# Attention scores of a two-layer trunk: q and k in rounded hi/lo parts, or in plain fp32 on either half of the partitions

## The chip, the cores and the metric

The kernel runs on one core of a Trainium2 chip. The metric is the device time of one execution in microseconds (us); lower is better. A change under about 2% can't be told from no change with certainty.

## What is computed

A decoder trunk of two layers on one sequence of 1024 positions with model width 1024, all in fp32. Layer 0 mixes tokens by a gated MLP in chunks, layer 1 by attention; each is followed by a squared-ReLU MLP of width 4096. The change is in the attention, of which this is the core (16 heads of width 64; three branches g, each with its own q, k and v; window and dilation (128, 1), (512, 4), (2048, 16)):

```python
def dilated_branch(q, k, v, window, dilation, slopes):
    span = window // dilation
    ...
    qb = to_blocks(q)
    kb = with_prev(to_blocks(k))        # the block before and the block itself
    vb = with_prev(to_blocks(v))
    s = jnp.einsum('bnqrhe,bnkrhe->bnrhqk', qb, kb,
                   preferred_element_type=jnp.float32) * (E ** -0.5)
    ...
    s = s + bias
    s = jnp.where(valid[None, :, None, None], s, NEG)
    m = jnp.max(s, axis=-1, keepdims=True)
    p = jnp.exp(s - m)
    l = jnp.sum(p, axis=-1, keepdims=True)
    o = jnp.einsum('bnrhqk,bnkrhe->bnqrhe', p / l, vb.astype(jnp.float32))
    lse = (m + jnp.log(l))[..., 0].transpose(0, 1, 4, 2, 3)
```

The span is 128 positions in each branch. The three outputs are then weighted by a softmax over their `lse` and added.

## The kernel before, in words

**Number formats.** Large products run in the rounded format fp32r. To keep precision, an operand is split: `split(hi, lo, src)` (L100) lets ScalarE (ACT) write the rounded part `hi` (L102) and VectorE (DVE) the remainder `lo = src - hi` (L103). A product is then three matmuls, hi·hi, hi·lo and lo·hi.

**The stages.** `mixer_a`, `mlp(1)`, `attention`, the output rows, and `mlp(3)` follow one another. The two MLPs take most of the time (L782, L938).

**The attention stage** handles 8 head pairs `hp`, and for each the branches g = 2, 1, 0: 24 groups. Two streams of work are woven together.

- `project()` is a generator. For each group it computes q, k and v of the head pair for the two halves of the positions, into PSUM banks of kind `mm` (two). For each of 8 k-steps it issues three 512-column matmuls (L1134) and yields. After the last k-step the bank, which holds the pair's two heads on partitions 0 to 63 and 64 to 127, is evicted: v by a copy on ACT (L1141), q and k by the lines that change. Positions are reordered by `perm` and `by_pos`, so that each branch finds its blocks side by side.
- `attend(n, …)` puts the attention work of a group into slots, eight to a group, four for each head `e`. `scores(m)` treats query tiles 2m and 2m+1 of 128 queries each. A tile sees its own 128 keys, and also the 128 before where `has[t]` is true (256 keys): all tiles but the first in branch 0, the odd tiles in branch 1, none in branch 2. The scores lie in PSUM banks of kind `sc` (two). DVE adds the bias and takes the row minimum of the negated scores (L1214), ACT takes the exponential and the sum (L1216). `transposes(m)` turns the probabilities by TensorE (L1239, L1242) and splits them; `weighted(m)` multiplies them with v (L1262), and ACT and DVE evict the sums (L1279, L1280).

The main loop goes through the slots. A slot has two parts, scores with weighted values, and transpositions; behind each part come three steps of `project()`, nine 512-column matmuls. When the projections are used up, in the last group, the first steps of the output projection (`begin`) take their place. The framework orders instructions by a planner of its own, except those that are pinned by `keep_in_program_order`.

**q and k before.** For each head `e` there are tiles `q{e}`, `k{e}` of 128 partitions in fp32r, two buffers each, and four fixed tiles `qlo[e][b]`. With the head's own 64 partitions called `mine` and the others `other`, `k{e}` holds hi on `mine` and lo on `other`; `q{e}` holds hi on `mine`, and GpSimd (POOL) copies it to `other` when both halves are there (L1150); `qlo` holds lo on `mine` and zeros on `other`, cleared once at the start (L1064). A score tile is two matmuls over all 128 partitions into one group: `q{e}` with `k{e}` (L1207) gives hi·hi + hi·lo, and `qlo` with `k{e}` (L1208) gives lo·hi. Both tiles of a `scores(m)` lie in one bank, side by side.

Of the kernel before, what the change touches and what calls it, by code (L numbers as in the profile page):

```python
# [10 lines left out]
F32 = mybir.dt.float32  # L11
F32R = mybir.dt.float32r
AF = mybir.ActivationFunctionType
ALU = mybir.AluOpType
# [3 lines left out]
P = 128  # L18
S = 1024
# [16 lines left out]
def trunk(ctx: ExitStack, tc: tile.TileContext, x, c, ada_w, ada_b, ln_g, ln_b, a_w_in, a_b_in,  # L36
# [4 lines left out]
    V, A, G, T = nc.vector, nc.scalar, nc.gpsimd, nc.tensor  # L41

    def pool(stack, name, bufs, **kw):
        return stack.enter_context(tc.tile_pool(name=name, bufs=bufs, reuse_waits="tile", **kw))
# [52 lines left out]
    def bank(kind, name):  # L97
        return ps[kind].tile([P, HALF], F32, name=name, tag=kind)

    def split(hi, lo, src, hi_engine=A, lo_engine=V):  # L100

        first = A.copy(hi, src) if hi_engine is A else hi_engine.tensor_copy(hi, src)  # L102
        return first, lo_engine.tensor_tensor(lo, src, hi, op=ALU.subtract)  # L103
# [943 lines left out]
    def attention(before):  # L1047
# [6 lines left out]
        with ExitStack() as ph:  # L1054
            open_psum(ph, "B", sc=2, pv=2, mm=2, tr=2)
            vec = pool(ph, "vecB", 1)
            gate = row_tile(gate_dram[2], "gate_2", "gate")
            ql = pool(ph, "attn_qlo", 1)
            qk = pool(ph, "attn_qk", 2)
            qp = pool(ph, "attn", 2)  # L1060
            qlo = [[ql.tile([P, S], F32R, name=f"qlo{e}_{b}") for b in range(2)] for e in range(2)]
            for e in range(2):
                for b in range(2):
                    (V if b else G).memset(qlo[e][b][64 - 64 * e : P - 64 * e, :].bitcast(F32), 0.0)  # L1064


            near = qp.tile([P, 2 * P], F32, name="near", bufs=1)
            G.iota(near[:], pattern=[[-1, 2 * P]], base=P, channel_multiplier=1, allow_small_or_imprecise_dtypes=True)
# [8 lines left out]
            def perm(t, g, half=None):  # L1077

                d = DILATION[g]
                if g == 0:  # L1080
                    return t if half is None else t[:, half * HALF : (half + 1) * HALF]
                if g == 1:
                    v = t.rearrange("p (r i) -> p r i", r=d)
                    n = v.shape[2] // 2
                else:
                    v = t.rearrange("p (a b i) -> p a b i", b=2, i=S // d)
                    n = v.shape[3] // 2
                return v[..., half * n : (half + 1) * n]

            def by_pos(t, g):  # L1090

                if g == 0:
                    return t
                if g == 1:
                    return t.rearrange("p (i r) -> p r i", r=4)
                return t.rearrange("p (i b a) -> p a b i", b=2, a=8)

            order = [(hp, g) for hp in range(N_PAIRS) for g in (2, 1, 0)]
            got = [dict() for _ in order]

            def project():

                todo = [(n, X) for n in range(len(order)) for X in range(3)]
                parts = [(n, X, half) for half in (1, 0) for n, X in todo[:4]]
                parts += [(n, X, half) for n, X in todo[4:] for half in (1, 0)]
                build = before.build(0)

                def load(n, X):
                    hp, g = order[n]
                    c0 = g * 3 * D + X * D + hp * P  # L1110
                    return unit(b_w_qkv[0, :, c0 : c0 + P], f"w{'qkv'[X]}_{hp}_{g}")

                units = {key: load(*key) for key in todo[:4]}
                for n, X, half in parts:
                    if (n, X, half) == (0, 0, 0):
                        run(build)
                    hp, g = order[n]
                    nm = "qkv"[X]
                    i = 3 * n + X
                    if half == 1 and 3 <= i < len(todo) - 1:  # L1120
                        units[todo[i + 1]] = load(*todo[i + 1])
                    if half == 1:
                        if nm == "v":
                            got[n]["vT"] = vec.tile([P, S], F32, name=f"vT_{hp}_{g}", tag="lnb")
                        else:
                            if nm == "q":
                                got[n]["qlo"] = [qlo[e][n % 2] for e in range(2)]
                            for m in ((f"{nm}0", f"{nm}1")):
                                got[n][m] = qk.tile([P, S], F32R, name=f"{m}_{hp}_{g}", tag=m)
                    wu = units[n, X]  # L1130
                    p = bank("mm", f"ps{nm}_{hp}_{g}_{half}")
                    for k in range(KD):
                        for c_, (a, b) in enumerate(((0, 0), (0, 1), (1, 0))):
                            T.matmul(p[:], wu[a][:, k * P : (k + 1) * P], hT[half][b][:, k, :],  # L1134
                                     start=k + c_ == 0, stop=k == KD - 1 and c_ == 2)
                        if half == 1 and (n, X) in ((0, 2), (1, 0)) and k % 2:
                            next(build, None)
                        if k == KD - 1:
                            src = by_pos(p[:], g)
                            if nm == "v":  # L1140
                                A.copy(perm(got[n]["vT"][:], g, half), src)  # L1141
                            else:
                                for e in range(2):
                                    mine, other = slice(64 * e, 64 * e + 64), slice(64 - 64 * e, P - 64 * e)
                                    t = got[n][f"{nm}{e}"]
                                    hi = perm(t[mine, :], g, half)
                                    lo = perm(got[n]["qlo"][e][mine, :] if nm == "q" else t[other, :], g, half)
                                    split(hi, lo, by_pos(p[mine, :], g))
                                    if nm == "q" and half == 0:
                                        G.tensor_scalar(t[other, :], t[mine, :], 1.0, 1.0, ALU.mult, ALU.mult)  # L1150
                        yield


# [14 lines left out]
            def attend(n, oT_of):  # L1168
                hp, g = order[n]
                base = 8 * n  # L1170
                my = got[n]
                has = [(g == 0 and t > 0) or (g == 1 and t % 2 == 1) for t in range(NT)]
                width = P if g == 2 else 2 * P
# [12 lines left out]
                for e in range(2):  # L1186
                    h = 2 * hp + e
                    rows = slice(e * HEAD, (e + 1) * HEAD)
                    probs, pvs, st = {}, [], dict(begun=[False, False])

                    def scores(m, e=e, h=h, rows=rows, probs=probs, st=st):
                        if m == 0:
                            if e == 0:
                                my["stat"] = qp.tile([P, 2, 2, NT], F32, name=f"stat_{hp}_{g}", tag="stat", bufs=3)
                            st["bias"] = qp.tile([P, width], F32, name=f"bias_{h}_{g}", tag="bias")
                            G.tensor_scalar(st["bias"][:], (far if g == 2 else near)[:],
                                            -8.0 * DILATION[g] * 2.0 ** (-8.0 * (h + 1) / N_HEADS), 1.0, ALU.mult, ALU.mult)
                        scb, used = bank("sc", f"sc_{h}_{g}_{m}"), 0
                        stat = my["stat"]
                        spans = []  # L1200
                        for t in (2 * m, 2 * m + 1):
                            w = 2 * P if has[t] else P
                            sl = slice(used, used + w)
                            used += w
                            k0 = (t - 1) * P if has[t] else t * P
                            tq, keys = slice(t * P, (t + 1) * P), my[f"k{e}"]
                            T.matmul(scb[:, sl], my[f"q{e}"][:, tq], keys[:, k0 : k0 + w], start=True, stop=False)  # L1207
                            T.matmul(scb[:, sl], my["qlo"][e][:, tq], keys[:, k0 : k0 + w], start=False, stop=True)  # L1208
                            spans.append((t, w, sl))
                        for t, w, sl in spans:  # L1210
                            pr = qp.tile([P, 2 * P], F32, name=f"p_{h}_{g}_{t}", tag="p", bufs=4)
                            col = (t % 2) * 4 + t // 2 if g == 1 else t
                            nm, l = stat[:, 0, e, col : col + 1], stat[:, 1, e, col : col + 1]
                            V.tensor_tensor_reduce(out=pr[:, 0:w], in0=scb[:, sl], in1=st["bias"][:, width - w :], scale=-0.125, scalar=3e38,  # L1214
                                                   op0=ALU.add, op1=ALU.min, accum_out=nm)
                            A.activation(pr[:, 0:w], pr[:, 0:w], AF.Exp, bias=nm, scale=-1.0, accum_out=l)  # L1216
                            probs[t] = pr
# [216 lines left out]
    out = attention(done)  # L1434
# [31 lines left out]
```

## Time and profile before

| | |
|---|---|
| time, two runs | 2842.47 and 2847.93 us, median 2845.2 |
| profiled execution, first to last instruction | span 2841.6 us (its own time is not given apart) |
| TensorE (PE) busy | 2752.7 us, 97% |
| VectorE (DVE), ScalarE (ACT) busy | 1944.5 us, 1413.9 us |
| first and last score matmul | 1045.3 and 2115.3 us |
| score matmuls, L1207 and L1208 | 384 and 384 |

The page gives the busy time of each engine, its share of 40 slices of the span, the chain of work that ended last and the costliest groups of instructions. PE is the matmul stream and PEld the weight loads beside it; matmul durations overlap, so a matmul's price is read from the distance between two starts. In a group, "out<-in" names tiles by the program's names, then come rows*columns of the weights, the shape, the count, busy us and mean ns of one, and the idle time before with what ended it. In a line in order of time, the first number is the start, the second the duration, both in us.

### The profile page before, as it was taken

Reading aid. Unit: us, or ns where it says so; the run is one execution under the profiler, and the core shown is the slowest. Engines: PE = TensorE matmul, PEld = TensorE weight load, DVE = VectorE, ACT = ScalarE, POOL = GpSimd, SP = SyncE. Lnnn points to the kernel's source line nnn. Section 1 sums busy time; section 2 is a strip of 40 time slices with the busy share of each in tenths; the row PEclk is TensorE's granted clock in tenths of the full one; section 3 lists DMA queues with packets and bytes.
Section 4 is the critical chain, followed back from the end, with each engine's and each line's share of the span. In section 5 each row is a group of like instructions: output and inputs, shape, how many; then the busy total and the mean of one; then the engine's idle time right before and its main releaser. Section 6 shows DMA issues by size and latency. Waiting matters only on the chain.

```text
span 2841.6 us, 36856 instructions
## 1 busy us (share of the span) xinstructions
PE 2752.7 (97%) x13290; PEld 2277.9 (80%) x13290; DVE 1944.5 (68%) x3485; ACT 1413.9 (50%) x2613; POOL 220.1 (8%) x163
## 2 busy tenths in 40 slices
PE   6999999999999999999999999999999999999997
PEld 5777878887888878888888888888877788878886
DVE  6786798777877674656555555555659976577776
ACT  3334375555434455555555555555564755544431
POOL 1021000000000043101000000010201000000000
PEclk9999999999999999999999999999999999999999
DMA  7533346668846343212121212121315564485561
GB/s 253 171 109 106 119 152 223 216 219 277 286 153 201 126 148 105 61 39 68 38 61 39 69 31 69 38 69 31 91 39 178 170 208 158 151 303 189 171 214 60
DMA packets 300186, 384.15 MB, mean 135 GB/s; under 512 B 47532, under 2 KB 172884, under 8 KB 300004
## 3 DMA queue, kind: packets, MB, share of 16 engines
q1 hardware_dynamic: 300004, 381.80, 42.0%
q8 instruction: 104, 1.70, 0.2%
q14 instruction: 78, 0.64, 0.1%
HBM read 297.77 MB, written 83.97 MB: 134 GB/s over the span
## 4 chain that ended last, share of the span: by engine, by line
PE 73%; DVE 11%; DMA 7%; ACT 5%; issue 2%; POOL 2%; SPq 0%; DVEq 0%; ACTq 0%; POOLq 0%
PE psd L938 21%; PE psua L782 10%; PE psv L1134 8%; PE psq L1134 7%; PE psk L1134 5%; PE psuc L782 5%; DMA adaw<-in_ada_w_dram 3%; PE psd_wout L356 3%; PE psub L782 2%; PE pv L1262 2%; PE psd_wo L356 2%; ACT p L1216 1%; DVE adaacc L128 1%; PE psu L356 1%; PE sc L1208 1%
## 5 line engine op out<-in xcount | busy, mean ns | idle before, releaser
L782 PE MATMUL psua<-right,left 128*128 128x512 f32 x1536 | 364.0, 391 | 3.4 <-ACT right L102 1.8
L938 PE MATMUL psd<-rhi,lhi 128*128 128x512 f32 x896 | 351.0, 392 | 2.1 <-ACT part L813 2.1
L938 PE MATMUL psd<-rlo,lhi 128*128 128x512 f32 x896 | 350.9, 392 | 1.2 <-DVE rlo L103 1.1
L938 PE MATMUL psd<-rhi,llo 128*128 128x512 f32 x896 | 350.5, 391 | 0.0
L782 PEld LDWEIGHTS psua<-right,left 128*128 128x128 f32 x1536 | 287.3, 188 | 65.5 <-DVE right L103 3.1
L1216 ACT ACTIVATE p<-p,stat 128x128 f32<-128x128 f32 (+1 forms) x384 | 170.4, 445 | 237.6 <-DVE stat L1214 235.7
L1134 PE MATMUL psv<-hT,wv_hi 128*128 128x512 f32 x768 | 246.0, 401 | 3.2 <-DVE qlo L103 3.2
L1134 PE MATMUL psq<-hT,wq_hi 128*128 128x512 f32 x768 | 246.3, 402 | 0.0
L1134 PE MATMUL psk<-hT,wk_hi 128*128 128x512 f32 x768 | 246.0, 401 | 0.0
L103 DVE TENSOR_TENSOR pTlo<-pT,pThi 128x512 fp32r<-128x512 f32 (+1 forms) x160 | 98.2, 621 | 179.1 <-ACT pThi L102 178.5
L938 PEld LDWEIGHTS psd<-rhi,lhi 128*128 128x128 f32 x896 | 169.3, 189 | 38.4 <-ACT part L813 2.9
L938 PEld LDWEIGHTS psd<-rlo,lhi 128*128 128x128 f32 x896 | 169.1, 189 | 37.0 <-DVE rlo L103 2.2
L938 PEld LDWEIGHTS psd<-rhi,llo 128*128 128x128 f32 x896 | 169.2, 189 | 35.3
L782 PE MATMUL psuc<-right,left 128*128 128x512 f32 x768 | 188.9, 392 | 0.0
L128 DVE SCALAR_TENSOR_TENSOR adaacc<-adaw,silu_c,adaacc 128x512 f32<-128x512 f32 x168 | 133.4, 805 | 64.1 <-DMA adaw<-in_ada_w_dram 63.4
L782 PEld LDWEIGHTS psuc<-right,left 128*128 128x128 f32 x768 | 144.4, 189 | 30.4 <-DVE right L103 0.5
L1214 DVE CUSTOM_DVE_ANT_0 p<-sc,bias 128x128 f32<-128x128 f32 (+1 forms) x384 | 119.7, 347 | 68.6 <-PE sc L1208 66.2
L1134 PEld LDWEIGHTS psv<-hT,wv_hi 128*128 128x128 f32 x768 | 135.6, 189 | 26.1 <-issue 2.8
L1134 PEld LDWEIGHTS psk<-hT,wk_hi 128*128 128x128 f32 x768 | 136.5, 189 | 22.6
L1134 PEld LDWEIGHTS psq<-hT,wq_hi 128*128 128x128 f32 x768 | 135.7, 189 | 22.2
L1134 PE MATMUL psq<-hT,wq_lo 128*128 128x512 f32 x384 | 151.4, 394 | 0.0
L1134 PE MATMUL psv<-hT,wv_lo 128*128 128x512 f32 x384 | 150.6, 392 | 0.0
(250 smaller groups left out, 5843.1 us busy)
## 6 DMA issues: line engine op xcount, KB each, us to landing
lraw<-forms SPq DMA_DIRECT2D x112, 512.0 KB, 3.7
adaw<-in_ada_w_dram SPq DMA_DIRECT2D x192, 256.0 KB, 3.2
up<-in_mlp_w_up_dram SPq DMA_DIRECT2D x64, 512.0 KB, 3.8
forms<-s SPq DMA_DIRECT2D x128, 256.0 KB, 2.4
rraw<-in_mlp_w_down_dram SPq DMA_DIRECT2D x64, 512.0 KB, 4.5
forms<-part SPq DMA_DIRECT2D x96, 256.0 KB, 2.5
spill<-acc SPq DMA_DIRECT2D x24, 512.0 KB, 2.7
wq_raw<-in_b_w_qkv_dram SPq DMA_DIRECT2D x24, 512.0 KB, 3.7
```

The costliest lines, as they stand in the source:

```text
L103: return first, lo_engine.tensor_tensor(lo, src, hi, op=ALU.subtract)
L128: ins = V.scalar_tensor_tensor(acc[:], raw[:], silu_c[:, k : k + 1], acc[:], ALU.mult, ALU.add)
L356: T.matmul(dst, s[a], m[b], start=(n == 0), stop=(n == last))
L782: T.matmul(acc, w[:, a, k, :], right[p][:, b, k, :], start=p in (1, 2, 5) and k + a + b == 0, stop=k == 3 and a == 1, skip_group_check=True)
L938: T.matmul(sums[kind, m][:], l[a][:, k, m * P : (m + 1) * P], r[b][:, k, :], start=p in (1, 5, 2, 3) and kp + k + a + b == 0, stop=kp == K ...
L1134: T.matmul(p[:], wu[a][:, k * P : (k + 1) * P], hT[half][b][:, k, :], start=k + c_ == 0, stop=k == KD - 1 and c_ == 2)
L1208: T.matmul(scb[:, sl], my["qlo"][e][:, tq], keys[:, k0 : k0 + w], start=False, stop=True)
L1214: V.tensor_tensor_reduce(out=pr[:, 0:w], in0=scb[:, sl], in1=st["bias"][:, width - w :], scale=-0.125, scalar=3e38, op0=ALU.add, op1=ALU.m ...
L1216: A.activation(pr[:, 0:w], pr[:, 0:w], AF.Exp, bias=nm, scale=-1.0, accum_out=l)
L1262: T.matmul(pvs[b][:, q0 % HALF : q0 % HALF + w_], stt, x_[:, o_ : o_ + w_], start=not begun[b], stop=left[b] == 0, skip_group_check=True)
```

## The change

q and k of a head are no longer split. ACT copies the projected values from PSUM to `mine`, and DVE copies the same values to `other`, both in plain fp32. A score tile becomes one plain fp32 matmul over 64 partitions: even tiles use partitions 0 to 63, odd tiles 64 to 127. Each tile has an `sc` bank of its own, so a `scores(m)` takes both banks. `qlo`, its clearing and POOL's copy go. The pools `attn` and `attn_qk` are opened in the other order.

```diff
-            ql = pool(ph, "attn_qlo", 1)
+            qp = pool(ph, "attn", 2)
             qk = pool(ph, "attn_qk", 2)
-            qp = pool(ph, "attn", 2)
-            qlo = [[ql.tile([P, S], F32R, name=f"qlo{e}_{b}") for b in range(2)] for e in range(2)]
-            for e in range(2):
-                for b in range(2):
-                    (V if b else G).memset(qlo[e][b][64 - 64 * e : P - 64 * e, :].bitcast(F32), 0.0)
...
-                            if nm == "q":
-                                got[n]["qlo"] = [qlo[e][n % 2] for e in range(2)]
                             for m in ((f"{nm}0", f"{nm}1")):
-                                got[n][m] = qk.tile([P, S], F32R, name=f"{m}_{hp}_{g}", tag=m)
+                                got[n][m] = qk.tile([P, S], F32, name=f"{m}_{hp}_{g}", tag=m)
...
-                                    hi = perm(t[mine, :], g, half)
-                                    lo = perm(got[n]["qlo"][e][mine, :] if nm == "q" else t[other, :], g, half)
-                                    split(hi, lo, by_pos(p[mine, :], g))
-                                    if nm == "q" and half == 0:
-                                        G.tensor_scalar(t[other, :], t[mine, :], 1.0, 1.0, ALU.mult, ALU.mult)
+                                    src = by_pos(p[mine, :], g)
+                                    A.copy(perm(t[mine, :], g, half), src)
+                                    V.tensor_copy(perm(t[other, :], g, half), src)
...
-                        scb, used = bank("sc", f"sc_{h}_{g}_{m}"), 0
...
                             w = 2 * P if has[t] else P
-                            sl = slice(used, used + w)
-                            used += w
+                            scb = bank("sc", f"sc_{h}_{g}_{t}")[:, 0:w]
+                            own = slice(64 * (t % 2), 64 * (t % 2) + 64)
                             k0 = (t - 1) * P if has[t] else t * P
-                            tq, keys = slice(t * P, (t + 1) * P), my[f"k{e}"]
-                            T.matmul(scb[:, sl], my[f"q{e}"][:, tq], keys[:, k0 : k0 + w], start=True, stop=False)
-                            T.matmul(scb[:, sl], my["qlo"][e][:, tq], keys[:, k0 : k0 + w], start=False, stop=True)
-                            spans.append((t, w, sl))
-                        for t, w, sl in spans:
+                            T.matmul(scb, my[f"q{e}"][own, t * P : (t + 1) * P], my[f"k{e}"][own, k0 : k0 + w],
+                                     start=True, stop=True)
+                            spans.append((t, w, scb))
+                        for t, w, scb in spans:
```

The DVE instruction of L1214 then reads `scb` in place of `scb[:, sl]`.

More of the change, by code (lines that the diff above doesn't have):

```diff
@@ L1213, in scores @@
                             nm, l = stat[:, 0, e, col : col + 1], stat[:, 1, e, col : col + 1]
-                            V.tensor_tensor_reduce(out=pr[:, 0:w], in0=scb[:, sl], in1=st["bias"][:, width - w :], scale=-0.125, scalar=3e38,
+                            V.tensor_tensor_reduce(out=pr[:, 0:w], in0=scb, in1=st["bias"][:, width - w :], scale=-0.125, scalar=3e38,
                                                    op0=ALU.add, op1=ALU.min, accum_out=nm)
```

## The prediction

> **What bounds the kernel now.** I read the page first, for the engine that fills the span and the chain that ends last.
>
> ```profile
> span 2841.6 us, 36856 instructions
> ...
> PE 2752.7 (97%) x13290; PEld 2277.9 (80%) x13290; DVE 1944.5 (68%) x3485; ACT 1413.9 (50%) x2613; POOL 220.1 (8%) x163
> ...
> PEclk9999999999999999999999999999999999999999
> ...
> PE 73%; DVE 11%; DMA 7%; ACT 5%; issue 2%; POOL 2%; SPq 0%; DVEq 0%; ACTq 0%; POOLq 0%
> ```
>
> TensorE (PE) is busy for 97% of the span, at full clock, and is 73% of the chain. The change touches only the attention stage, whose scores run from 1045 to 2115 us. So next come the stage's busy times and PE's own waits in it (the second view from 1000 to 2130 us: engine, line, whom it waited for, us, times, longest).
>
> ```profile
> 1043.00:2125.00 1082.00, 1066.64 (x5740) 894.83 (x5739) 606.93 (x1465) 589.46 (x1400) 144.21 (x118) 1.00 0.22 59
> ```
>
> ```profile
> PE pv L1262 <- DVE pTlo L103: 4.1, 10, 0.5
> PE pT L1239 <- DVE v L103: 3.6, 8, 0.5
> PE psv L1134 <- DVE qlo L103: 3.2, 2, 2.4
> ```
>
> PE works 1066.64 of 1082.00 us; VectorE (DVE) 606.93, ScalarE (ACT) 589.46, GpSimd (POOL) 144.21. All PE idle time is 15.4 us, the most that earlier operands could give back. Anything larger must come from what the score instructions cost PE. Here they are by shape, busy and mean ns of one:
>
> ```profile
> L1208 PE MATMUL sc<-k,qlo 128*128 128x128 f32 x208 | 54.0, 275 | 0.0
> L1207 PE MATMUL sc<-k,q 128*128 128x256 f32 x176 | 51.7, 306 | 0.1
> L1208 PE MATMUL sc<-k,qlo 128*128 128x256 f32 x176 | 47.7, 282 | 0.0
> L1207 PE MATMUL sc<-k,q 128*128 128x128 f32 x208 | 46.8, 241 | 0.0
> ```
>
> These durations overlap, so the price is the distance between starts. In order of time (start, us), a block `scores(m)` of two query tiles that both see 256 keys, one of two 128-key tiles, and a mixed one:
>
> ```profile
> 1305.02 0.28 PE L1207 MATMUL sc<-k,q 128*128 128x256 f32 x1
> 1305.14 0.28 PE L1208 MATMUL sc<-k,qlo 128*128 128x256 f32 x1
> ...
> 1305.49 0.28 PE L1262 MATMUL pv<-pThi,v 128*128 128x256 f32 x1
> ```
>
> ```profile
> 1323.18 0.22 PE L1207 MATMUL sc<-k,q 128*128 128x128 f32 x1
> 1323.24 0.28 PE L1208 MATMUL sc<-k,qlo 128*128 128x128 f32 x1
> 1323.36 0.27 PE L1207 MATMUL sc<-k,q 128*128 128x128 f32 x1
> ...
> 1323.58 0.68 PE L1134 MATMUL psq<-hT,wq_hi 128*128 128x512 f32 x2
> ```
>
> ```profile
> 1360.99 0.22 PE L1207 MATMUL sc<-k,q 128*128 128x128 f32 x1
> ...
> 1361.45 0.23 PE L1262 MATMUL pv<-pThi,v 128*128 128x128 f32 x1
> ```
>
> A block takes 0.47, 0.40 and 0.46 us. A 128-column matmul behind another whose weights were ready starts 0.06 later, all others 0.11 to 0.12 whether 128 or 256 columns: here the weight load sets the pace, about 0.11 each.
>
> There are 8 head pairs x 3 dilations x 2 heads x 4 = 192 blocks. Dilation 0 gives one mixed and three wide blocks a head, dilation 1 four mixed, dilation 2 four narrow: 48 wide, 80 mixed, 64 narrow (48 x 2 + 80 = 176 matmuls of 256 columns, the count in the rows). The scores cost PE 48 x 0.47 + 80 x 0.46 + 64 x 0.40 = **85 us**, 3% of the kernel. Even if they were free, no more than 3% could be won.
>
> **The change, part by part.** *Scores.* Per tile, two fp32r matmuls over 128 rows (L1207, L1208) become one plain fp32 matmul over 64 rows. The trace has no such instruction, so I bound it. Below: it streams its columns once like any matmul here, one instruction for two, half of 85 us: -42; with the halves side by side, a quarter: -64. Against that stands the kernel's own arithmetic: it splits operands into hi and lo because one pass in fp32r loses bits, and spends three passes per product (L1134: hi.hi, hi.lo, lo.hi). A product that keeps both halves of both operands is four such passes inside the instruction, and nothing in 64 rows shares them out, as the stacked rows do now. That is the nearest row, so I take four. Its unit:
>
> ```profile
> 1319.78 0.39 PE L1134 MATMUL psq<-hT,wq_hi 128*128 128x512 f32 x1
> 1320.01 0.39 PE L1134 MATMUL psq<-hT,wq_lo 128*128 128x512 f32 x1
> 1320.24 1.03 PE L1182 MATMUL psvt<-ident,vT 128*128 128x128 f32 x8
> 1321.03 0.70 PE L1134 MATMUL psq<-hT,wq_hi 128*128 128x512 f32 x2
> ```
>
> 512 columns take 0.23. So a 256-key tile in four passes takes 0.46 and a 128-key tile 0.23 (estimates from this row). The Trainium skill, FP8 and Floating Point Precision, section TensorE Precision Notes, states the same count of four passes for true fp32; no run here shows it.
>
> *The two halves.* How far do an even tile in rows 0 to 63 and an odd one in rows 64 to 127 overlap? Three cases; weight loads stay four a block (hi and lo of two tiles), so a narrow block stays at 0.40 or more.
> - None: 0.92, 0.69, 0.46: 44.2 + 55.2 + 29.4 = 129 us, **+44**.
> - Partly: PE starts matmuls in order. If an instruction is two halves (weights hi, then lo, each streaming its columns twice), the odd tile can start only beside the even tile's second half. A wide block is three units of 0.23, 0.69; a mixed one 0.115 + 0.23 + 0.23 = 0.575; a narrow one 0.345, held to 0.40: 33.1 + 46.0 + 25.6 = 104.7, **+20**.
> - Full: 0.46, 0.46, 0.40: 84.5, **0**; if weights of the two halves also load side by side, the narrow block falls to 0.23, 73.6: -11.
>
> I take the middle case: the code puts odd tiles behind even ones and the trace shows matmul starts strictly in order.
>
> *Entering and leaving half rows.* Each block goes from 128-row work to 64-row work and back. The nearest row is the only matmul with a narrower shape, the 128x32 transposition of the statistics:
>
> ```profile
> 1180.91 0.39 PE L1134 MATMUL psq<-hT,wq_lo 128*128 128x512 f32 x1
> 1181.14 0.27 PE L1294 MATMUL pstat<-ident,stat 128*32 128x128 f32 x1
> 1181.17 0.31 PE L1207 MATMUL sc<-k,q 128*128 128x128 f32 x1
> ...
> 1181.64 0.34 PE L1262 MATMUL pv<-pThi,v 128*128 128x256 f32 x1
> ```
>
> From 1181.14 to 1181.64 lie that matmul and a narrow block: 0.50 - 0.40 = 0.10, no more than the 0.10 of a full transposition (1320.24 to 1321.03 for eight). So two changes of shape cost 0 to 0.10. Upper bound: the array must empty both times (a 512-column matmul is recorded 0.39 long while starts are 0.23 apart, so 0.16 each) and the next weights (0.11) can't load ahead: 2 x 0.27 x 192 = 104 us. I take half of the nearest row, 0.05 a block: **+10**.
>
> *Evictions of q and k (L1148).* ACT's cast becomes a copy, DVE's subtraction a copy, of the same 64x512 shapes.
>
> ```profile
> L103 DVE TENSOR_TENSOR k<-psk,k 64x512 fp32r<-64x512 f32 x93 | 64.1, 689 | 35.7 <-ACT k L102 32.5
> L102 ACT CAST k<-psk 64x512 fp32r<-64x512 f32 x93 | 54.0, 580 | 38.0 <-DVE k L103 21.5 <-PE psk L1134 15.1
> L1150 POOL TENSOR_SCALAR q<-q 64x1024 fp32r<-64x1024 f32 x48 | 61.1, 1273 | 295.7 <-ACT q L102 295.2
> L462 DVE COPY vz<-psvt 128x512 f32<-128x512 f32 x16 | 10.7, 685 | 3.8 <-PE psvt L461 3.8
> L1141 ACT COPY vT<-psv 128x512 f32<-128x512 f32 x47 | 27.4, 584 | 4.6 <-PE psv L1134 4.2
> ```
>
> Copies out of PSUM take 685 and 584 ns against 689 and 580: nothing on either engine. DVE no longer reads what ACT writes, so the bank may come free some 0.6 us sooner, but only 3.2 us of PE waits go back to that (`psv <- DVE qlo`): **-2**. POOL's 48 duplicates (61 us) and the clearing of `qlo` go; PE never waited for them: 0. The stage's DMAs are the same.
>
> *Banks.* A block now takes both `sc` banks, so its even matmul waits for DVE's read of the block before, with all of PE queued behind it. For the block of 1305.02:
>
> ```profile
> 1305.69 0.42 DVE L1214 CUSTOM_DVE_ANT_0 p<-sc,bias 128x256 f32<-128x256 f32 x1 [1.25 <-PE sc L1208]
> ...
> 1306.04 0.42 DVE L1214 CUSTOM_DVE_ANT_0 p<-sc,bias 128x256 f32<-128x256 f32 x1
> ...
> 1310.59 0.28 PE L1207 MATMUL sc<-k,q 128*128 128x256 f32 x1
> ```
>
> DVE has read both tiles by 1306.46, and the next block starts at 1310.59, so nothing while projections fill the slots. In the last slots fill is thin; I add 1 us (bounds 0 and the 15.4 us of idle doubled).
>
> Sum: 20 + 10 - 2 + 1 = **+29** on the profiled span: 2841.6 to 2871. The two timed runs (median 2845.2, 2842.47 to 2847.93) lie 0.9 to 6.3 above that span; added to the median it is **2874**.
>
> **The rivals.** About 2% (57 us) is what a measurement of this kernel can tell from no change.
> - *Full overlap, free switches*: 0 or -11, -2 for the waits: **2832 to 2845**. For: the banks are apart and 0.10 bounds both shape changes. Against: in-order starts. Chance 0.2.
> - *No overlap, cheap switches*: 44 + 10 - 1: **2898**. For: nothing in this trace shows two matmuls running beside each other in one array. Chance 0.25.
> - *Slower: the array empties at every change of shape.* Place: 192 blocks, twice each. Price 0.32 a block, 61 us, on the middle case: 20 + 61 - 1 = +80, **2925**; with weights exposed, 2968; on no overlap, 2949 and up. It decides from 0.20 a block on the middle case, from 0.07 with no overlap. The statistics row speaks against it, but that keeps all 128 rows. The Trainium skill, TensorEngine Tiling, section Tiling Modes (Key Properties), says that changing the mode, not just the tile, drains the engine; the 0.10 of the statistics row doesn't bear this out for a narrower output, and no run here shows it for fewer rows. Chance 0.18.
> - *The instruction is cheaper than four passes* (two: narrow blocks 0.40, wide 0.46 without overlap): 22.1 + 27.6 + 25.6 = 75, -10, 2835; one pass reaches 2781 to 2803. Against: the kernel's own three passes. Chance 0.07, of which 0.02 over 2% faster.
>
> Forecast, middle case: chance 0.3, **2874**. With the switches at 0 to 0.10 a block, its own range is 2864 to 2884. The range reaches down into full overlap and up into the emptying array: **2836 to 2926**. Slower by over 2% (above 2902): the emptying rival, 0.18, and a third of the no-overlap case with dearer switches: 0.25. Faster by over 2%: 0.02. Within 2%: 0.73.
>
> **What would show it.** In the new trace a wide score block should last about 0.69 from its first start to the next line's start, 0.46 under full overlap, 0.92 under none; starts of the odd tile tell which. A gap ahead of the first score matmul or behind the last, beyond 0.05 a block, shows the emptying. DVE and ACT busy time in the stage should stay within a few us of 606.93 and 589.46, POOL fall by about 61. PE waits on `sc` should be absent before 2100 us. The prediction fails if plain fp32 over 64 rows isn't four passes, if a shape change costs over 0.1, or if the order of PE's work around the scores comes out differently.

## The result, and the profile after

The changed kernel takes 2876.5 us (2873.4 and 2879.7) against 2845.2: a ratio of 1.0115, interval 1.0091 to 1.0140: slower in both of its runs, but by less than the 2% from which on a change counts as certain. Two executions at about two thirds of the clock, one of the kernel before and one of the kernel with two blocks at once below, are left out of all medians. The forecast was 2874. The time is right, but it comes out of terms that were wrong in opposite directions, as the lines show. The page of the changed kernel:

```profile
span 2871.6 us, 36756 instructions
...
PE 2800.0 (98%) x13290; PEld 2236.2 (78%) x13290; DVE 1951.7 (68%) x3483; ACT 1416.1 (49%) x2613; POOL 150.4 (5%) x113
...
PE 84%; DVE 10%; DMA 3%; ACT 1%; issue 1%; SPq 0%; DVEq 0%; POOL 0%; ACTq 0%; POOLq 0%
```

TensorE (PE) is still the bound, and its share of the chain has risen from 73% to 84%. The attention stage, its busy times from 1043 us to its end, and PE's own waits:

```profile
1043.00:2155.00 1112.00, 1109.07 (x5701) 847.56 (x5700) 612.59 (x1459) 587.70 (x1395) 81.38 (x71) 1.00 0.20 56
```

```profile
PE sc L1195 <- DVE stat L1202: 1.4, 7, 0.2
PE psv L1126 <- DVE mv L238: 0.9, 1, 0.9
PE pv L1250 <- DVE pTlo L103: 0.9, 2, 0.5
```

PE is idle for 2.9 us of the stage, where it was 15.4. VectorE (DVE) and ScalarE (ACT) are as before; GpSimd (POOL) has lost 63 us. Next, the ends of the stage: first projection matmul and last product with v, before and after.

```profile
999.99 0.62 PE L1134 MATMUL psq<-hT,wq_hi 128*128 128x512 f32 x2
...
2121.36 0.28 PE L1262 MATMUL pv<-pTlo,v 128*128 128x128 f32 x1
```

```profile
995.34 0.62 PE L1126 MATMUL psq<-hT,wq_hi 128*128 128x512 f32 x2
...
2151.96 0.28 PE L1250 MATMUL pv<-pTlo,v 128*128 128x128 f32 x1
```

The stage grew from 1121.4 to 1156.6 us, by 35. The 4.6 us that this execution was ahead at the stage's beginning lie in unchanged code. Now a wide score block (two tiles of 256 keys) in order of time, first as asked for from 1300.5 to 1300.8, then whole:

```profile
1300.23 0.39 PE L1126 MATMUL psv<-hT,wv_lo 128*128 128x512 f32 x1
1300.55 0.49 PE L1195 MATMUL sc<-k,q 64*128 64x256 f32 x2
```

```profile
1300.55 0.70 PE L1195 MATMUL sc<-k,q 64*128 64x256 f32 x4
1301.18 0.73 PE L1126 MATMUL psv<-hT,wv_hi 128*128 128x512 f32 x2
1301.74 0.40 PE L1126 MATMUL psv<-hT,wv_lo 128*128 128x512 f32 x1
```

Each plain fp32 matmul leaves two records, one for each set of weights. Views that end earlier or later count them: one has started by 1300.55, two by 1300.56, and the other two start between 1300.86 and 1300.88. The records don't say which tile they belong to. I read them as the even and the odd tile starting together, and then their second halves together: **full overlap**, not the partial one of the forecast (in the experiment without overlap, below, all four start one after the other, from 1331.96 to 1332.71, so the two halves of one tile don't start together). But the block isn't cheap. The 512 columns ahead of it need 0.23 us, to 1300.46; the scores start at 1300.55. After them, the first two projection matmuls take 0.56 (1301.18 to 1301.74) where two take 0.46 elsewhere. Counted from 1300.46 to 1301.28 (1301.74 less 0.46) the block costs **0.82**, against 0.47 before. The weight loads (PEld) say why:

```profile
1300.00 0.19 PEld L1126 LDWEIGHTS psv<-hT,wv_lo 128*128 128x128 f32 x1
1300.54 0.30 PEld L1195 LDWEIGHTS sc<-k,q 64*128 64x128 f32 x4 [0.35 <-issue]
1301.18 0.30 PEld L1126 LDWEIGHTS psv<-hT,wv_hi 128*128 128x128 f32 x2 [0.33 <-issue]
```

Before, the first score weights were loaded a matmul ahead (1304.79 for the scores of 1305.02):

```profile
1304.79 0.19 PEld L1207 LDWEIGHTS sc<-k,q 128*128 128x128 f32 x1
```

Now they start with the matmul that needs them, on entering and on leaving the 64-row shape, each time some 0.09 us after the columns ahead have streamed. So a change of shape costs a pause of 0.09, which I read as the array emptying, and 0.11 for a load that nothing covers, and a block pays that twice, 0.39. The rest, 0.43, is two streams of four passes over 256 columns beside each other. A narrow block:

```profile
1324.65 0.39 PE L1126 MATMUL psq<-hT,wq_lo 128*128 128x512 f32 x1
1324.97 0.49 PE L1195 MATMUL sc<-k,q 64*128 64x128 f32 x4
1325.39 0.73 PE L1126 MATMUL psq<-hT,wq_hi 128*128 128x512 f32 x2
1325.95 0.40 PE L1126 MATMUL psq<-hT,wq_lo 128*128 128x512 f32 x1
```

From 1324.88 to 1325.49 it costs 0.61, 0.39 of it for the shape. With mixed blocks as wide ones (the longer tile decides), the scores cost 128 x 0.82 + 64 x 0.61 = 144 us in place of 85. That is 59 more, while the stage grew by 35: over 20 us came back somewhere. That is the second question of the experiments.

### The profile page after: what moved, and what is told of

It is laid out like the page before. It is cut to its first block, busy times and chain, and to the rows that moved or that the text cites. A ratio compares the mean times of both kernels' runs of the same rounds, so it can differ in the third digit from the quotient of the medians.

```text
span 2871.6 us, 36756 instructions
## 1 busy us (share of the span) xinstructions
PE 2800.0 (98%) x13290; PEld 2236.2 (78%) x13290; DVE 1951.7 (68%) x3483; ACT 1416.1 (49%) x2613; POOL 150.4 (5%) x113
## 4 chain that ended last, share of the span: by engine, by line
PE 84%; DVE 10%; DMA 3%; ACT 1%; issue 1%; SPq 0%; DVEq 0%; POOL 0%; ACTq 0%; POOLq 0%
PE psd L938 20%; PE psua L782 10%; PE psq L1126 9%; PE psk L1126 9%; PE psv L1126 8%; PE psuc L782 5%; PE sc L1195 4%; PE pv L1250 4%; PE psd_wout L356 3%; PE psub L782 2%; PE psd_wo L356 2%; DMA adaw<-in_ada_w_dram 2%; PE psu L356 2%; PE pT L1227 2%; PE psv L453 1%; DVE adaacc L128 1%
## 5 line engine op out<-in xcount | busy, mean ns | idle before, releaser
L1126 PE MATMUL psk<-hT,wk_lo 128*128 128x512 f32 x384 | 151.0, 393 | 0.0
```

## The experiments

Theory S: the halves overlap fully, and every block pays 0.39 us for two changes of shape. Theory P: the forecast's.

**No change of shape.** All 128 partitions, in the changed kernel:

```diff
-own = slice(64 * (t % 2), 64 * (t % 2) + 64)
+own = slice(0, P)
-    -8.0 * DILATION[g] * ...
+    -16.0 * DILATION[g] * ...
...
-    scale=-0.125
+    scale=-0.0625
```

> The changed kernel, but every score matmul contracts over all 128 partitions. Both halves hold the same values, so the sum comes out doubled, and the bias is doubled and the scale halved to match. No change of shape in TensorE, and no two matmuls side by side. Theory S (the two halves overlap fully, and each block pays about 0.39 us for going to 64 rows and back: 0.09 until the array is empty and 0.107 for weights that can't load ahead, twice): a block goes from 0.82, 0.82, 0.61 us (wide, mixed, narrow) to four passes of each tile after the other, 0.85 to 0.92, 0.64 to 0.69, 0.43 to 0.46, so 144 us of scores become 120 to 129: 15 to 24 us less than the changed kernel, 2852 to 2862. Theory P (that of the forecast: half overlap, changes of shape at 0.05): 114 us become 129, 15 us more than the changed kernel, about 2891.

Measured: 2855.6 us, ratio to before 1.0042 (1.0026 to 1.0058), 21 less than the changed kernel. Its wide block:

```profile
1302.96 0.39 PE L1126 MATMUL psv<-hT,wv_lo 128*128 128x512 f32 x1
1303.19 1.02 PE L1195 MATMUL sc<-k,q 128*128 128x256 f32 x4
1303.86 0.81 PE L1126 MATMUL psv<-hT,wv_hi 128*128 128x512 f32 x2
1304.52 0.40 PE L1126 MATMUL psv<-hT,wv_lo 128*128 128x512 f32 x1
```

The format is plain fp32 here too, and there is no gap ahead (0.23 to the scores): it is the change of shape that brings the gap, not the format. And 1303.19 to 1304.06 (1304.52 less 0.46) is 0.87 for the two tiles one behind the other, within the 0.85 to 0.92 of S. P, which wanted 15 us more, falls. The whole is 21 us less, within the 15 to 24 of S. Using half the rows with full overlap is *slower* here than using all rows twice as long.

**No overlap.** `own = slice(0, 64)` for both tiles.

> The changed kernel, but even and odd tiles both contract over partitions 0 to 63; the banks stay apart. The change of shape stays, the overlap goes. Theory S (full overlap, 0.39 us a block for the shape): a block loses the shorter tile's cover, 0.43 us in a wide one, 0.21 in a mixed and a narrow one: 48 x 0.43 + 144 x 0.21 = 51 us more than the changed kernel, about 2927. Theory P (half overlap): 24 us more, about 2900. If the halves don't overlap at all: the same time, 2876.

Measured: 2926.1 us, ratio 1.0289 (1.0273 to 1.0305), 50 more than the changed kernel.

```profile
1331.63 0.40 PE L1126 MATMUL psq<-hT,wq_lo 128*128 128x512 f32 x1
1331.96 1.13 PE L1195 MATMUL sc<-k,q 64*128 64x256 f32 x4
1333.02 0.39 PE L1250 MATMUL pv<-pThi,v 128*128 128x256 f32 x1
```

The block lasts 1.06 from its first start to the next line's, where it lasted 0.63 (1300.55 to 1301.18): 0.43 more, the whole second tile. The overlap was full, and a tile's four passes over 256 columns are 0.43.

**Half as many changes of shape.** Two blocks at once, two tiles side by side in each bank:

```diff
-for t in (2 * m, 2 * m + 1):
-    scb = bank("sc", ...)[:, 0:w]
+both, used = [bank("sc", ...) for x in range(2)], [0, 0]
+for t in range(2 * m, 2 * m + 4):
+    scb = both[t % 2][:, used[t % 2] : used[t % 2] + w]
+    used[t % 2] += w
...
-for t, w, scb in spans:                     # the reads by DVE
+for t, w, scb in spans[-1:] + spans[:-1]:   # the last tile first
...
-for m in range(4):
+for m in range(0, 4, 2):
```

> The changed kernel, but the score matmuls of two neighbouring blocks are issued together, four tiles at a time, the two even ones side by side in one bank and the two odd ones in the other; eight buffers for the probabilities in place of four. Same matmuls, half as many changes of shape (96 blocks in place of 192). Theory S: 96 x 0.39 = 37 us less than the changed kernel, about 2839, if no new wait comes of it. Theory P (0.05 a block): 5 us less, about 2871. A third, that the banks are held too long: TensorE waits for VectorE at the score matmuls and the time rises.

Measured: 2853.0 us (median of six; the 2854 of a later expectation counts the one left out), ratio 1.0030 (1.0018 to 1.0042), 23 less than the changed kernel: the sign and most of the size of S, 14 us short. Most of that is in PE's waits, where the changed kernel had none at the transpositions of the probabilities:

```profile
PE pT L1232 <- DVE v L103: 7.4, 8, 0.9
...
PE pT L1232 <- ACT p L1209: 3.9, 8, 0.5
```

That is 11 us, in 16 places, two in each head pair. In one of the longer ones TensorE waits for DVE's part of the split of v, which stands behind ACT's:

```profile
1362.15 1.08 ACT L102 CAST v<-psvt 128x512 fp32r<-128x512 f32 x2
...
1363.98 0.33 PE L1232 MATMUL pT<-ident,p 128*128 128x128 f32 x1 [0.92 <-DVE v L103]
```

Ahead of that cast ACT worked through the exponentials of four tiles in a row (1358.79 to 1361.08) and a copy of sums. So the work of four tiles at once can stand ahead of what the next transposition needs; the other places weren't followed up in this way.

**More PE time, nothing else.** Where did over 20 us come back? Theory W: later scores wait less. In the kernel before, L1207 twice:

```diff
+T.matmul(scb[:, sl], my[f"q{e}"][:, tq], keys[:, k0 : k0 + w], start=True, stop=True)
 T.matmul(scb[:, sl], my[f"q{e}"][:, tq], keys[:, k0 : k0 + w], start=True, stop=False)
```

> The kernel before, with the first of the two score matmuls of each tile issued twice (the second time it starts the sum anew, so the result stays). It adds 384 matmuls of about 0.11 us to TensorE, 42 us, and changes nothing else. Theory W (time that TensorE spends more in the scores is partly given back, since operands that it waited for, transposed probabilities above all, are then ready in time; about 20 us of this stage): 2845 + 22 = 2867. Without W: 2887.

Measured: 2898.1 us, ratio 1.0185 (1.0167 to 1.0204): 53.5 more, beyond both. More PE time brought nothing back; waits grew. PE's wait at the transpositions, before and here:

```profile
PE pT L1239 <- ACT p L1216: 2.7, 10, 0.6
```

```profile
PE pT L1240 <- ACT p L1217: 18.2, 16, 2.4
```

Weight loads for the transpositions, before (first two rows) and here:

```profile
PEld pT L1242 <- ACT p L1216: 9.6, 22, 0.7
...
PEld pT L1239 <- ACT p L1216: 8.4, 22, 0.8
```

```profile
PEld pT L1240 <- ACT p L1217: 25.8, 25, 2.6
PEld pT L1243 <- ACT p L1217: 8.7, 28, 0.5
```

W falls. So the waits went for another reason: the banks (theory B) or the evictions (theory E).

**The banks alone.** The kernel before, each tile's two matmuls in a bank of its own:

```diff
-scb, used = bank("sc", f"sc_{h}_{g}_{m}"), 0
...
-    sl = slice(used, used + w)
-    used += w
+    scb = bank("sc", f"sc_{h}_{g}_{t}")[:, 0:w]
```

> The kernel before, with one part of the change: each query tile's two score matmuls go into a bank of their own, so that a block takes both banks. The question is what took away the waits of TensorE in the changed kernel (the stage's idle time fell from 18.5 to 3.9 us, and the transposed probabilities from 64.7 to 53.1 us of TensorE's time). Theory B (the banks: VectorE may read the even tile while the odd one is still being made, so the probabilities are ready sooner): 10 to 15 us less than before, 2830 to 2835. Theory E (the evictions of q and k, where VectorE no longer waits for ScalarE): no change, 2845. Theory B': holding both banks makes TensorE wait for VectorE's reads: more than 2845.

Measured: 2837.8 us, ratio 0.9983 (0.9974 to 0.9992), 5 less than the 2843.3 beside it. And the other way round, one bank in the 128-row kernel:

> The kernel that contracts over all 128 partitions (2855.6 us), with both tiles of a block in one bank again. Theory B (the banks took the waits away): 10 to 15 us more, 2866 to 2871. Theory E (the evictions did): no change, 2856.

Measured: 2861.2 us, ratio 1.0067 (1.0050 to 1.0085) against 1.0042 with two banks: about 6 us more by the medians, though the two intervals overlap. Both signs fit B, with a third to a half of the size that it was given; E's "no change" is missed by as much.

**The evictions alone.** In the changed kernel:

```diff
-V.tensor_copy(perm(t[other, :], g, half), src)
+V.tensor_copy(perm(t[other, :], g, half), perm(t[mine, :], g, half))
```

> The changed kernel, but VectorE copies q and k to the other half from what ScalarE has just written, not from PSUM, so it waits for ScalarE again as in the kernel before. Theory E (free evictions took the waits away): 10 to 15 us more than the changed kernel, 2886 to 2891. Theory B: no change, 2876.

Measured: 2889.6 us, ratio 1.0162 (1.0141 to 1.0183): 13 more than the changed kernel, as E has it, though DVE is busy 36 us less in the stage, since copies out of SBUF are shorter (576.34 against 612.59):

```profile
1043.00:2172.00 1129.00, 1116.60 (x5727) 851.20 (x5726) 576.34 (x1464) 594.59 (x1400) 84.20 (x71) 1.00 0.20 57
```

The wait of the transpositions' weight loads, in the changed kernel and here:

```profile
PEld pT L1227 <- ACT p L1204: 2.3, 10, 0.3
```

```profile
PEld pT L1227 <- ACT p L1204: 15.8, 28, 1.4
```

That wait is back. So evictions that don't chain are worth about 13 us and the banks about 5: most of what came back. The 13 has a wide margin, some 9 us either way by the two intervals, for the changed kernel was timed only twice. The length of the stage in the profiled executions agrees: 11 us more with chained copies (1000.83 to 2168.89), 4 less with the banks alone (996.28 to 2114.11), 8 more with one bank again (998.06 to 2140.90, after 1002.52 to 2137.76). The end of POOL's copies and the other order of the pools weren't tested alone. How an eviction's order reaches the transpositions (through the queues of ACT and DVE, and a planner that orders them anew in each kernel) wasn't traced further and stays open.

**Towards a better version.** First, blocks together without the new waits (the probabilities also get twelve buffers in place of eight):

```diff
-n_t = 2 * (2)
+n_t = 2 * (4 if g == 2 else 2)
...
-when = [0, 1, 2, 3]        # branch 1
+when = [1, 1, 2, 3]
```

> The kernel that issues two score blocks together (2854 us), with two changes: in the branch without a key block before, all four blocks of a head go together (16 groups in place of 32), and in the middle branch the first transposition of the probabilities is moved one slot later, since TensorE waited there 0.46 to 0.93 us twice in each head pair (16 places, 11 us). Theory S: 16 x 0.39 = 6 us and the 11 us of waits less: 2837, below the kernel before. If the waits only move to the next place: 2848.

Measured: 2846.8 us, ratio 1.0014 (1.0005 to 1.0024). The waits moved, as the second reading has it: products with v, which hardly waited before (first row), now wait.

```profile
PE pv L1255 <- DVE pTlo L103: 0.7, 2, 0.5
```

```profile
PE pv L1255 <- DVE pTlo L103: 6.3, 15, 0.5
```

Then the 64-row shape only where it is cheap: branch 2, eight narrow tiles for one change of shape. Branches 1 and 0 as before the change, with a bank for each tile.

```diff
+if g == 2:                                  # evictions
+    A.copy(perm(t[mine, :], g, half), by_pos(p[mine, :], g))
+    V.tensor_copy(perm(t[other, :], g, half), by_pos(p[mine, :], g))
+    continue
...
+for t in range(8 if g == 2 else 0):         # scores, once a head
+    scb = both[t % 2][:, t // 2 * P : t // 2 * P + P]
+    own, tq = slice(64 * (t % 2), 64 * (t % 2) + 64), slice(t * P, (t + 1) * P)
+    T.matmul(scb, my[f"q{e}"][own, tq], my[f"k{e}"][own, tq], start=True, stop=True)
```

> The two middle branches as in the kernel before, with a bank for each tile (2837.8 us); only the third branch (128 keys a tile) as changed, with plain fp32 over either half of the partitions, all eight tiles of a head issued together, the four even ones in one bank and the four odd ones in the other. Theory S: a head's third-branch scores cost four blocks of 0.40 to 0.45 us before; together they cost one change of shape, 0.39, and 4 x 0.213 us of passes, 1.24: 16 x 0.36 to 0.56 = 6 to 9 us less, and up to 4 us of waits less since a third of the evictions no longer chain: 2825 to 2832, below both kernels. Against it: eight reads of VectorE in a row, with the transpositions one slot behind, may bring new waits: 2838 or more.

Measured: 2836.8 us, ratio 0.9972 (0.9962 to 0.9982): below both kernels, by 0.28% and 1.4%, each under the 2% from which on a change counts as certain. From the kernel with the banks alone it can't be told apart (0.9983, and the intervals overlap). The stage itself did get shorter. Its first projection matmul and last product with v, with the banks alone and here:

```profile
996.28 0.62 PE L1134 MATMUL psq<-hT,wq_hi 128*128 128x512 f32 x2
...
2114.11 0.27 PE L1260 MATMUL pv<-pTlo,v 128*128 128x128 f32 x1
```

```profile
1002.95 0.62 PE L1134 MATMUL psq<-hT,wq_hi 128*128 128x512 f32 x2
...
2115.01 0.27 PE L1279 MATMUL pv<-pTlo,v 128*128 128x128 f32 x1
```

From 1117.83 to 1112.06 us it lost 5.8, close to the 6 to 9 of the passes; the 4 us of waits didn't come, since waits only moved from the transpositions to the products with v (again with the banks alone, then here):

```profile
PE pT L1237 <- ACT p L1214: 7.2, 9, 2.3
...
PE pv L1260 <- DVE pTlo L103: 1.8, 4, 0.5
```

```profile
PE pv L1279 <- DVE pTlo L103: 6.4, 17, 0.6
...
PE pT L1256 <- ACT p L1233: 1.9, 7, 0.3
```

Why the medians show 1 us of the 5.8 stays open: outside the stage, in lines that the edit leaves alone, these two executions took 1715.4 and 1724.9 us.

## Why the prediction was right, and where it wasn't

- **PE is the bound, nothing over 3% to win**: right; DVE, ACT and POOL did what was forecast.
- **Four passes**: right. 0.43 for 256 columns (the block without overlap) against the 0.46 estimated. The count that the Trainium skill gives in FP8 and Floating Point Precision, TensorE Precision Notes, agrees with that.
- **The two halves, +20**: the step that failed first. I took the odd tile to start beside the even one's second half, because matmuls started in order. They do not across halves: the odd tile's first half starts with the even one's. Streams of 0.43, 0.43 and 0.21 make 68.5 us, 16 *less* than the 85. The rival of full overlap had this part. The forecast's own sign would have misled here: a wide block lasts 0.63 from its first start to the next line's, which looks like the 0.69 of half overlap, but it is 0.43 of streams, 0.11 of the first load and 0.09 of pause. The Trainium skill, TensorE: Matmul & The Clock Gate, Part 3 (Packing small matmuls), has tiles in different rows starting a few ns apart; the trace agrees, with one start by 1300.55 and both by 1300.56.
- **Entering and leaving half rows, +10**: the term that was mis-sized most. 0.05 a block measured 0.39, or 75 us. I went by the narrow transposition, which keeps all 128 rows, and gave the emptying rival 0.18. Its price, 0.32 to 0.54, held the truth. The Trainium skill, TensorEngine Tiling (Array Packing), Tiling Modes (Key Properties), says that a change of mode drains the engine. The pause of 0.09 us on either side agrees with that; the load that can't run ahead, 0.11 us a side, came on top.
- **Evictions, -2, and banks, +1**: about -13 and -5. I counted the waits on the evicted bank and not those of the transpositions. The waits on `sc` that the forecast had as absent before 2100 us came to 1.4 us, in seven places before 2051 us.
- **The sum**: -16 + 75 - 13 - 5 = 41 against the 35 of the stage, and 31 between the medians; forecast, 20 + 10 - 2 + 1 = 29. A narrow block before costs nearer 0.45 than 0.40 with the first two matmuls behind it (1323.58, 0.68 long), 3 of the 6 that are over; the rest is unexplained. The forecast came out by luck: an overlap that was better than expected, and waits that went, paid for shape changes that were dearer. No case of it had full overlap and dear shape changes together.

## What to carry to other kernels

Half-height matmuls in pairs may overlap fully and still lose: price the change of shape on both sides (here 0.39 us a visit, as much as the pair's own work), and try several blocks in one visit (two at once brought 23 us here of an expected 37, and new waits took 11 of the rest). A 64-row product needs neighbours of its own shape, not only a partner in the other half. When PE is 97% busy, its remaining waits still move the time by about 5 to 13 us with the order of evictions and banks; test such a part alone before you credit or blame the arithmetic.

## What the hardware showed that I had not expected

The two row halves run as two streams: the odd tile's first half starts ahead of the even tile's second, though the even tile comes first in the program. A copy that chained on another engine's result was cheaper for DVE (36 us less busy) and still made the kernel 13 us slower.
